# Norm sums of a DeltaNet head in four column strips, its 32x32 products of both chunks in turn, and z's last step emitted later

## The chip, the core and the metric

The kernel runs on one core of a Trainium2 chip. Such a core has a matrix engine (TensorE, PE in the profile; PEld is its loading of weights), a vector engine (VectorE, DVE), a scalar engine (ScalarE, ACT), a general one (GpSimd, POOL) and SyncE (SP), whose queue issues this kernel's DMAs. Each engine works through its own list of instructions in a fixed order and waits at an instruction whose operands are not there yet. The metric is the device time of one execution in microseconds (us), lower is better.

## The reference

One layer of a hybrid encoder block in float32, 1024 positions, width 1024: RMSNorm, one input projection, two mixers (a gated DeltaNet with 4 heads of 128, and a banded chunk attention), gates, output projection, a convolved feed-forward part, and a last RMSNorm. The change lies in the DeltaNet mixer:

```python
qa = l2norm(qa.reshape(b_, t_, GDN_HEADS, GDN_DK))
ka = l2norm(ka.reshape(b_, t_, GDN_HEADS, GDN_DK))
...
a_mat = beta[..., :, None] * jnp.einsum('nbhid,nbhjd->nbhij', k, k) * dec_strict
sol = lax.linalg.triangular_solve(a_mat + eye, rhs, left_side=True, lower=True)
...
oa = (rmsnorm(oa, gdn_norm_w[l]) * jax.nn.silu(za))
```

Positions are worked on in 16 chunks of 64. In each chunk a unit lower triangular 64x64 system is solved, and a state S of 128x128 is carried from chunk to chunk. The norm of q is not applied to q: since the output is normalised too, it is folded into the last RMSNorm, for which the sum of squares of q at each position is needed (sx in the kernel).

## The kernel before

**Stages.** All products are made as three matmuls of split operands (high and low parts), accumulated in PSUM. After the first loads (up to about 64 us) comes the DeltaNet stage (to about 440 us), then attention, the branch products, the output projection and the feed-forward part. In the DeltaNet stage PE has two kinds of work: *fill*, the input projections (psph, 24 matmuls of 128x512 to a half tile of 512 positions, one weight tile of `load_w` for two halves), and the heads' own products.

**One head.** Two chunks of 64 lie in one tile of 128 partitions, so 8 pairs (NT = 8), with chunk e = 0 or 1 in partitions 64e to 64e+63. `gdn_prep` and `gdn_prep2` transpose k and v (psk, psv), make the decays, and the 64x64 products psG and psQ, with the two chunks of a pair in two strips of 64 columns of the array, alternately. `gdn_solve` inverts the four 32x32 diagonal blocks on DVE, 31 dependent steps on tmp and Zt; the result goes to HBM (dZ) and comes back by four loads, one for each block, into the tile zt. `gdn_apply` (line 541) makes the remaining 32x32 block of each chunk's inverse: Z11 is a transposed copy, psB1 a product of 32x32 for each pair, copied by ACT to B1, psZ21 a second product, copied by ACT into zt. Then come psW and psU, with zt as operand. `gdn_chain` carries the state through 16 steps: psws, then U on DVE, then pss, then S on DVE; after every second step pso and O.

**q's norm.** `gdn_qnorm` (line 610) squares q on ACT (sqq, 128 x 8 x 128) and puts eight small matmuls (psn, one column each, sqq as weights) into the list `side`; `proj_half` issues one of them after each three psph. `gdn_qnorm2` copies psn to sx with two ACT copies. `gdn_rms` (line 627) uses sx on DVE (line 634) and scales O; `gdn_out` transposes O (psoT), multiplies by z and stores to dO.

**z.** `gdn_z` (line 597) makes silu of the output gate, by halves e: psph times rb on DVE (line 604), tanh on ACT (zth, line 605), and a last step on DVE, (zth + 1) x zs (line 606).

**The order.** The program is traced head by head (from line 665), the head's own work at high priority; a scheduler then sets each engine's order by priorities and by when it expects operands. The tables APP, QN, GFILL, OUT and others at the top of the file say at which half tile of the fill the apply, the norm sums and the output are emitted. `behind()` puts PE's instructions of a piece behind the last matmul traced with `mm`.

The page and the trace name tiles without trailing numbers: psB1 is psB, psZ21 is psZ, Z11 is Z, zt0 is zt.

## Time and profile before

| | |
|---|---|
| time, median of 3 runs | 1549.16 us (1548.48 to 1549.85) |
| the profiled execution's own time | 1549.47 us |
| its span, first to last instruction | 1547.7 us |
| mean granted clock of PE over the span | 0.997 |
| DeltaNet stage, 64 to 440 us: PE, DVE, ACT, POOL busy | 370.10, 257.95, 174.78, 115.96 us of 376 |

A line of the profile names the source line, the engine, the operation, and the tiles written and read (out<-in). In a list of waits the three numbers are the total in us, how often, and the longest. In a timeline a line gives start and duration in us, and in square brackets idle time of the engine just before and what ended it; equal neighbours are merged (x16). Matmuls are pipelined, so their durations overlap, and the distance of their starts is what they cost.

### The profile page before, as it was taken

To read this page: it belongs to the slowest core of one execution; us is meant where nothing else is said; L and a number is where in the kernel's file an instruction comes from. 1 tells how busy PE (TensorE), PEld (TensorE's weight loads), DVE (VectorE), ACT (ScalarE), POOL (GpSimd) and SP (SyncE) were. 2 spreads that over 40 slices of the span, in tenths; PEclk is the share of its full clock that TensorE was granted. 3 is DMA by queue.
4 is the path that set the end of the run, shared out by engine and by line. 5 is a ranking of instruction groups with operands and counts; after the bars stand their busy time and mean duration, and the time that the engine had idled before them with its cause. 6 is when DMAs were issued, how large, how long until landed. Compare 5 with 4: busy or idle time off the path is not lost.

```text
span 1547.7 us, 21371 instructions
## 1 busy us (share of the span) xinstructions
PE 1517.9 (98%) x7687; PEld 1245.4 (80%) x7687; DVE 1091.1 (70%) x2146; ACT 716.4 (46%) x1408; POOL 640.8 (41%) x603
## 2 busy tenths in 40 slices
PE   8999999999999999999999999999999999999997
PEld 6878787877778888887887888888888888878886
DVE  7775867948436877866554567777777777797886
ACT  7644526363225665754232245444444444443344
POOL 3633323312132112111320269877777776233253
PEclk9999999999999999999999999999999999999999
DMA  8122131222131101114553213333333332875523
GB/s 301 31 64 83 45 103 32 64 71 82 49 126 50 37 23 59 37 55 138 173 168 122 95 56 116 117 102 103 102 102 103 102 102 76 277 253 164 178 89 141
DMA packets 74507, 162.04 MB, mean 105 GB/s; under 512 B 15649, under 2 KB 16929, under 8 KB 74401
## 3 DMA queue, kind: packets, MB, share of 16 engines
q1 hardware_dynamic: 74400, 160.68, 31.4%
q8 instruction: 60, 0.98, 0.3%
q14 instruction: 47, 0.38, 0.1%
HBM read 120.55 MB, written 40.11 MB: 104 GB/s over the span
## 4 chain that ended last, share of the span: by engine, by line
PE 54%; DVE 1%; DMA 1%; issue 0%; ACT 0%; POOL 0%; POOLq 0%; SPq 0%; DVEq 0%; ACTq 0%
PE psd L52 9%; PE psph L52 8%; PE pb L52 8%; PE pa L52 5%; PE psout L52 5%; PE pc L52 5%; PE psd L1511 4%; PE pb L1156 4%; PE pa L1156 3%; PE pc L1156 3%; PE pso L52 1%; PE pst L1044 0%; PE psp L877 0%; DMA tb<-dG 0%; DMA woraw<-w_out 0%
## 5 line engine op out<-in xcount | busy, mean ns | idle before, releaser
L84 POOL TENSOR_TENSOR wlo<-wraw,whi 128x256 fp32r<-128x256 f32 x196 | 157.3, 832 | 441.6 <-ACT whi L81 268.7
L52 PE MATMUL psph<-BH,whi 128*128 128x512 f32 x688 | 280.4, 407 | 7.9 <-ACT BH L225 5.2
L52 PE MATMUL psph<-BL,whi 128*128 128x512 f32 x688 | 276.0, 401 | 0.1
L52 PE MATMUL psph<-BH,wlo 128*128 128x512 f32 x688 | 275.5, 400 | 0.0
L52 PEld LDWEIGHTS psph<-BH,whi 128*128 128x128 f32 x688 | 130.7, 190 | 30.1 <-ACT BH L225 5.6
L1170 POOL TENSOR_TENSOR ol<-wraw,oh 128x512 fp32r<-128x512 f32 x110 | 150.5, 1386 | 6.6 <-ACT oh L1170 6.5
L52 PEld LDWEIGHTS psph<-BL,whi 128*128 128x128 f32 x688 | 130.6, 190 | 22.9 <-DVE BL L226 2.1
L52 PEld LDWEIGHTS psph<-BH,wlo 128*128 128x128 f32 x688 | 130.5, 190 | 22.7
L1170 POOL TENSOR_TENSOR al<-araw,ah 128x1024 fp32r<-128x1024 f32 (+1 forms) x28 | 69.4, 2481 | 132.9 <-ACT ah L1170 108.0
L52 PE MATMUL psd<-wdl,ah 128*128 128x512 f32 (+1 forms) x311 | 120.6, 388 | 1.4 <-DVE wdl L1170 1.4
L1170 POOL TENSOR_TENSOR wraw<-wraw 128x512 f32<-128x512 f32 x86 | 119.2, 1386 | 4.9
L1511 PE MATMUL psd<-wdh,al 128*128 128x512 f32 (+1 forms) x311 | 120.4, 387 | 0.0
L52 PE MATMUL psd<-wdh,ah 128*128 128x512 f32 (+1 forms) x311 | 119.4, 387 | 0.0
L1170 ACT CAST oh<-wraw 128x512 fp32r<-128x512 f32 x110 | 67.8, 620 | 103.9 <-POOL wraw L1170 103.8
L1170 DVE TENSOR_TENSOR wdl<-W,wdh 128x512 fp32r<-128x512 f32 x77 | 95.0, 1272 | 27.6 <-ACT wdh L1170 27.5
L81 ACT CAST whi<-wraw 128x1024 fp32r<-128x1024 f32 (+2 forms) x61 | 55.3, 907 | 79.5 <-PE psph L52 66.0
L1170 ACT CAST ah<-araw 128x1024 fp32r<-128x1024 f32 (+1 forms) x39 | 40.6, 1040 | 107.1 <-PE psd L52 52.8
L1170 POOL TENSOR_TENSOR gl<-wraw,gh 128x512 fp32r<-128x512 f32 x42 | 56.2, 1342 | 68.7 <-ACT gh L1170 68.7
L52 PEld LDWEIGHTS psd<-wdl,ah 128*128 128x128 f32 x311 | 58.4, 188 | 14.2 <-DVE wdl L1170 2.2
L1156 PE MATMUL pa<-BH,gh 128*128 128x512 f32 x176 | 68.6, 389 | 0.0
L52 PE MATMUL pa<-BH,gl 128*128 128x512 f32 x176 | 68.5, 389 | 0.0
L52 PE MATMUL pa<-BL,gh 128*128 128x512 f32 x176 | 68.5, 389 | 0.0
(343 smaller groups left out, 3802.6 us busy)
## 6 DMA issues: line engine op xcount, KB each, us to landing
wraw<-w_up SPq DMA_DIRECT2D x44, 512.0 KB, 5.0
wraw<-w_tiles SPq DMA_DIRECT2D x42, 512.0 KB, 3.5
araw<-dA SPq DMA_DIRECT2D x77, 256.0 KB, 3.0
dA<-yu SPq DMA_DIRECT2D x33, 512.0 KB, 3.1
W<-w_down SPq DMA_DIRECT2D x44, 256.0 KB, 4.5
xt<-x SPq DMA_DIRECT2D x16, 512.0 KB, 4.8
dG<-gt SPq DMA_DIRECT2D x16, 512.0 KB, 2.8
ta<-dG SPq DMA_DIRECT2D x16, 256.0 KB, 3.0
```

What stands on the lines that cost most here:

```text
L52: last["mm"] = nc.tensor.matmul(*args, **kw).ins
L81: nc.scalar.copy(hi, src)
L84: nc.gpsimd.tensor_tensor(out=lo[:, k:k + 2], in0=src[:, k:k + 2], in1=hi.bitcast(F32)[:, k:k + 2], op=ALU.subtract)
L1156: i = nc.tensor.matmul(ps, wh[:, k], xh[:, k], start=start and k == 0, stop=False, **kw)
L1170: return lambda *args, **kw: tc.keep_in_program_order(f(*args, **kw))
L1511: i = nc.tensor.matmul(ps, al[:, j, ts], wh[:, es], start=False, stop=stop, **kw)
```

## The change

**Norm sums.** In place of eight products with sqq as weights and a single moving column there are four with 32 columns of ones as weights and 256 columns of sqq moving, each into its own strip of 32 PSUM partitions (psn is 128 x 256; all 32 rows of a strip are alike). They are one entry of `side`, issued together. ACT copies psn to sn, which shares the buffer of the tile B1; one DMA stores a row of each strip to HBM (dN), and two DMAs load it back, position by position, to sx (64 partitions x 8 single floats each).

**32x32 products.** `gdn_apply` now makes both chunks' transposes first, then the psB1 products of both chunks in turn, both copies, the psZ21 products in turn, both copies. The four loads of zt are issued in the order of blocks 1, 3, 0, 2.

**z.** The last step of a half is emitted later: that of e = 0 after the tanh of e = 1, that of e = 1 after the first half tile of the fill behind it.

The tile `ones` goes, and `mhalf` is wider.

```diff
-        for b in range(4):
+        for b in (1, 3, 0, 2):
             r = slice(b * 32, (b + 1) * 32)
             nc.sync.dma_start(zt[r, :, r], dZ[b].rearrange("n a c -> a n c"))
...
-        for e in range(2):
-            r0 = slice(e * CH, e * CH + 32)
-            r1 = slice(e * CH + 32, (e + 1) * CH)
+        rr = [(slice(e * CH, e * CH + 32), slice(e * CH + 32, (e + 1) * CH)) for e in range(2)]
+        for r0, r1 in rr:
             nc.vector.transpose(out=Z11[r0], in_=zt[r0, :, r0])
-            for p in range(NT):
+        for p in range(NT):
+            for r0, r1 in rr:
                 mm(psx1[r0, p * 32:(p + 1) * 32], nL[r1, p, 0:32], zt[r1, p, r1], start=True, stop=True)
+        for r0, r1 in rr:
             nc.scalar.copy(B1[r0].rearrange("p n j -> p (n j)"), psx1[r0, 0:256])
-            for p in range(NT):
+        for p in range(NT):
+            for r0, r1 in rr:
                 mm(psx2[r0, p * 32:(p + 1) * 32], Z11[r0, p, :], B1[r0, p, :], start=True, stop=True)
+        for r0, r1 in rr:
             nc.scalar.copy(zt[r0, :, r1], psx2[r0, 0:256].rearrange("p (n j) -> p n j", j=32))
...
-            nc.vector.scalar_tensor_tensor(out=zs[:, s], in0=th, scalar=1.0, in1=zs[:, s], op0=ALU.add, op1=ALU.mult)
+            if e:
+                c["zf"]()
+
+            def zf(th=th, s=s):
+                with behind():
+                    nc.vector.scalar_tensor_tensor(out=zs[:, s], in0=th, scalar=1.0, in1=zs[:, s], op0=ALU.add,
+                                                   op1=ALU.mult)
+
+            c["zf"] = zf
             yield
...
-        psn = psc.tile([P, 8], F32, tag="c", name="psn")
-        for p in range(NT):
-            side.append(lambda p=p: mm(psn[:, p:p + 1], sqq[:, p, :], ones, start=True, stop=True))
+        psn = psc.tile([P, 256], F32, tag="c", name="psn")
+
+        def sums():
+            for j in range(4):
+                mm(psn[j * 32:(j + 1) * 32], ones2[:, 0:32], sqq[:, 2 * j:2 * j + 2, :].rearrange("p n t -> p (n t)"),
+                   start=True, stop=True)
+
+        side.append(sums)
...
-        psn = c["psn"]
+        sn = gp.tile([P, 256], F32, tag="B1", name="sn")
+        nc.scalar.copy(sn, c["psn"])
+        dN = gd.tile([4, 256], F32, tag="dN", name="dN")
+        nc.sync.dma_start(dN, sn[0:P:32, :])
         sx = gp.tile([P, NT], F32, tag="sx", name="sx", bufs=2)
         for e in range(2):
-            nc.scalar.copy(sx[(1 - e) * CH:(2 - e) * CH], psn[e * CH:(e + 1) * CH])
+            nc.sync.dma_start(sx[(1 - e) * CH:(2 - e) * CH, :],
+                              bass.AP(tensor=dN.tensor, offset=dN.offset + e * CH, ap=[[1, CH], [P, NT]]))
...
             got = next(fill, "end") != "end"
+            if n == 0 and h >= 0:
+                cs[h]["zf"]()
```

**In PE's order**, first head, from the psph ahead of the first 32x32 products up to psW (psB and psZ are the two products, Z and B their operands), before:

```order
L52 MATMUL psph<-BH,wlo 128x512
L52 MATMUL psB_1273<-zt_289,nL 32x32 x8
L52 MATMUL psph<-BH,whi 128x512
L52 MATMUL psph<-BL,whi 128x512
L52 MATMUL psph<-BH,wlo 128x512
L52 MATMUL psZ_1275<-B_1274,Z_1272 32x32 x8
L52 MATMUL psB_1273<-zt_289,nL 32x32 x8
L52 MATMUL psph<-BH,whi 128x512
L52 MATMUL psph<-BL,whi 128x512
L52 MATMUL psph<-BH,wlo 128x512
L52 MATMUL psZ_1275<-B_1274,Z_1272 32x32 x8
```

and with the change:

```order
L52 MATMUL psph<-BH,wlo 128x512
L52 MATMUL psB_1271<-zt_287,nL 32x32 x16
L52 MATMUL psph<-BH,whi 128x512
L52 MATMUL psph<-BL,whi 128x512
L52 MATMUL psph<-BH,wlo 128x512
L52 MATMUL psZ_1273<-B_1272,Z_1270 32x32 x16
L52 MATMUL psph<-BH,whi 128x512
L52 MATMUL psph<-BL,whi 128x512
L52 MATMUL psph<-BH,wlo 128x512
L52 MATMUL psph<-BH,whi 128x512
L52 MATMUL psW<-zt_287,nKs 128x128 x4
```

Three groups among the psph have become two; the second and third head are alike. In the last head each of the two is torn: one psB alone, three psph, fifteen psB, three psph, one psZ alone, three psph, fifteen psZ. The psn rows were one after each third psph (in the last head all eight together); they are four together now in all heads. Between the last pso and the psoT of the last head stand 24 psph, where 16 stood.

**In DVE's order**, last head, from the end of the solve into the chain (the tile sx holds the sums, U and S are the chain's steps), before:

```order
L523 TENSOR_REDUCE Zt<-tmp 128x8
L176 TENSOR_TENSOR gt<-psph,rb 128x512
L634 TENSOR_SCALAR sx<-sx 128x8
L547 STREAM_TRANSPOSE Z_3812<-zt_289 32x256
L604 TENSOR_TENSOR zs<-psph,rb 128x512
L547 STREAM_TRANSPOSE Z_3812<-zt_289 32x256
L606 SCALAR_TENSOR_TENSOR zs<-zth,zs 128x512
L584 TENSOR_TENSOR U<-psws,U 64x128
```

and with the change:

```order
L521 TENSOR_REDUCE Zt<-tmp 128x8
L174 TENSOR_TENSOR gt<-psph,rb 128x512
L544 STREAM_TRANSPOSE Z_3810<-zt_287 32x256 x2
L605 TENSOR_TENSOR zs<-psph,rb 128x512
L612 SCALAR_TENSOR_TENSOR zs<-zth,zs 128x512
L585 TENSOR_TENSOR U<-psws,U 64x128
L586 TENSOR_SCALAR O<-psws,eg 64x128
L590 SCALAR_TENSOR_TENSOR S<-S,eg,pss 128x128
L652 TENSOR_SCALAR sx<-sx 128x8
L585 TENSOR_TENSOR U<-psws,U 64x128
```

The operation on sx has moved behind the chain's first step; z's last step stands where it stood, right ahead of the first U. Of the eight places of z's last step (four heads, two halves), five stand at the same step of the chain as before, and the others one to three steps later.

**In SP's order**, last head, before (dZ and zt are the solve's result, dG a gate's store, wraw a weight tile):

```order
L531 DMA dZ<-Zt 128x256
L180 DMA dG<-gt 128x1024
L536 DMA zt_289<-dZ 32x8x32 x4
L92 DMA wraw<-w_tiles 128x1024 x2
L180 DMA dG<-gt 128x1024
```

and with the change:

```order
L529 DMA dZ<-Zt 128x256
L534 DMA zt_287<-dZ 32x8x32 x4
L178 DMA dG<-gt 128x1024
L90 DMA wraw<-w_tiles 128x1024
L638 DMA dN<-sn 4x256
L641 DMA sx<-dN 64x8x1 x2
L90 DMA wraw<-w_tiles 128x1024
L178 DMA dG<-gt 128x1024
```

The loads of zt have moved ahead of the gate's store, and the three new transfers stand between two weight loads.

## The prediction

> **What bounds the kernel now.** I read the page first, then the busy time by stage, then what TensorE (PE) waited for, and last the timeline of PE around the instructions that the change touches.

> ```profile
> PE 1517.9 (98%) x7687; PEld 1245.4 (80%) x7687; DVE 1091.1 (70%) x2146; ACT 716.4 (46%) x1408; POOL 640.8 (41%) x603
> 64.00:440.00 376.00, 370.10 (x2302) 298.55 (x2301) 257.95 (x669) 174.78 (x447) 115.96 (x165) 1.00 0.20 64
> PE pss L52 <- DVE U L584: 3.1, 5, 1.2
> ```

> The second line is the DeltaNet stage, where all of the change lies: 376 us long, PE busy for 370.10 of it, DVE for 257.95, the granted clock 1.00. The third is the longest wait of PE on another engine there: 3.1 us in five pieces. So PE is the bound, its order is fixed, and it hardly waits: microseconds of PE work that go there come off the end, as long as no wait grows in their place.

> Busy time of PE is a poor measure of what a matmul costs, since matmuls overlap (one psph lasts 0.39 us, but the next starts after 0.227). I therefore measure cost by starts: the time from the last ordinary psph ahead of a piece of work to the second psph behind it, less an interval for each psph in that stretch. The first fence gives the interval (PE alone, start and duration in us; 66 intervals lie between its last two lines).

> ```profile
> 102.22 0.39 PE L52 MATMUL psph<-BH,wlo 128*128 128x512 f32 x1
> 102.45 0.28 PE L52 MATMUL psn<-ones,sqq 128*128 128x1 f32 x2
> ...
> 109.34 0.40 PE L52 MATMUL psph<-BL,whi 128*128 128x512 f32 x1
> ...
> 111.85 0.39 PE L52 MATMUL psph<-BH,whi 128*128 128x512 f32 x1
> ...
> 126.81 0.39 PE L52 MATMUL psph<-BH,whi 128*128 128x512 f32 x1
> ```

> The interval is (126.81 - 111.85) / 66 = 0.227 us.

> **The norm sums: what goes.** In the first head eight psn products lie among 23 intervals: 109.34 - 102.22 = 7.12, less 23 x 0.227 = 5.22, leaves 1.90 us, 0.24 each, for a product with a single moving column: the load of its 128 columns of weights is what is paid. The order of heads two and three is the same. In the last head the eight stand in a row:

> ```profile
> 385.70 0.39 PE L52 MATMUL psph<-BH,wlo 128*128 128x512 f32 x1
> 385.92 1.84 PE L52 MATMUL psn<-ones,sqq 128*128 128x1 f32 x16
> 387.62 0.48 PE L52 MATMUL psph<-BH,whi 128*128 128x512 f32 x1
> 387.94 0.39 PE L52 MATMUL psph<-BL,whi 128*128 128x512 f32 x1
> ```

> 387.94 - 385.70 - 2 x 0.227 = 1.79 us. Removed in all: 3 x 1.90 + 1.79 = 7.49. (The second line also shows that one float32 product is two records: eight give x16.)

> **The 32x32 products: what goes.** First head, PE alone:

> ```profile
> 127.26 0.39 PE L52 MATMUL psph<-BH,wlo 128*128 128x512 f32 x1
> 127.58 0.69 PE L52 MATMUL psB<-zt,nL 32*32 32x32 f32 x16
> ...
> 128.54 0.40 PE L52 MATMUL psph<-BL,whi 128*128 128x512 f32 x1
> 128.77 0.39 PE L52 MATMUL psph<-BH,wlo 128*128 128x512 f32 x1
> 129.09 0.59 PE L52 MATMUL psZ<-B,Z 32*32 32x32 f32 x13
> 129.50 0.21 PE L52 MATMUL psB<-zt,nL 32*32 32x32 f32 x1
> 129.52 0.19 PE L52 MATMUL psZ<-B,Z 32*32 32x32 f32 x1
> ...
> 130.45 0.39 PE L52 MATMUL psph<-BL,whi 128*128 128x512 f32 x1
> ...
> 131.00 0.69 PE L52 MATMUL psZ<-B,Z 32*32 32x32 f32 x16
> ```

> The first group of eight costs 128.54 - 127.26 - 0.45 = 0.83. The middle sixteen cost 130.45 - 128.77 - 0.45 = 1.23. The last eight look like the first (0.69 for x16): 0.83. Together 2.89 us a head. Within a group a record starts every (0.69 - 0.19) / 15 = 0.033 us, so 16 records are 0.53 of the 0.83, and 0.30 is the price of entering and leaving such a group.

> The middle lines hold the key. In program order all eight psZ products (rows and columns 0 to 31) stand ahead of psB's second eight (another corner of the array). Yet a psB starts at 129.50, before psZ at 129.52: where two corners have work in the queue, they run abreast, each at its own pace. With the chunks alternating, 32 records take 16 steps: 16 x 0.033 + 0.30 = 0.83 for psB, and the same for psZ: 1.66 a head, a saving of 1.23. In the last head the order tears each group in two, one product alone and fifteen behind the next three psph: 2 x (2 x 0.033 + 0.30 + 15 x 0.033 + 0.30) = 2.32, a saving of 0.57. Sum: 3 x 1.23 + 0.57 = 4.26 us. Bounds: nothing saved if corners did not overlap, which those lines exclude, and a little more if the groups' entries shrink.

> **The norm sums: what comes.** Four products now, each 128 rows by 32 columns of weights with 256 moving columns, into four column strips. No such form is in this trace; the nearest are these (first two lines: two strips of 64 columns taken alternately; last two: full width, 128 moving columns).

> ```profile
> 71.61 0.92 PE L52 MATMUL psG<-kf 128*64 128x64 f32 x24
> 72.36 1.10 PE L52 MATMUL psQ<-WQ,kf 128*64 128x64 f32 x32
> ...
> 132.42 1.05 PE L52 MATMUL psW<-zt,nKs 128*128 128x128 f32 x8
> 133.31 1.06 PE L52 MATMUL psU<-Vs,zt 128*128 128x128 f32 x8
> ```

> A full-width record of 128 columns takes (133.31 - 132.42) / 8 = 0.111 us, so one of 64 would take 0.056; psG takes (72.36 - 71.61) / 24 = 0.031. Two strips therefore run abreast almost without loss. A record of 256 columns takes 0.22. Four strips abreast: 2 x 0.22 + 0.30 = 0.74 us a head. Two abreast: 4 x 0.22 + 0.30 = 1.18. One after another: 8 x 0.22 + 0.30 = 2.06, a small loss. I take 0.90, nearer to the first, since psG shows no sign of a limit at two; it is charged four times, 3.60. The sums net 7.49 - 3.60 = 3.89 us saved, between -0.8 and 4.5.

> [...]

> **The transposes of the last head.** In the order, 24 psph now stand between the last pso and psoT of the last head, where 16 stood. These are PE's timeline there, and an answer on the tile psoT (engine and line waited for, us, times):

> ```profile
> 437.53 2.35 PE L649 MATMUL psoT<-ident,O 128*128 128x128 f32 x8
>   ACT O L641: 1.2, 7
> ```

> PE waited 1.2 us in seven pieces for ACT to scale O. Eight more psph, 1.8 us, are ahead of it now, so I count 1.2 as gained; it is between 0 and 1.2.

> **z's last step.** All waits of that step, and one of them on DVE and what it did to PE:

> ```profile
> DVE zs L606 <- ACT zth L605: 4.7, 7, 1.4
> 347.94 0.69 DVE L606 SCALAR_TENSOR_TENSOR zs<-zth,zs 128x512 f32<-128x512 f32 x1 [1.37 <-ACT zth L605]
> 349.02 0.49 PE L52 MATMUL pss<-U,Kd 128*128 128x128 f32 x2 [1.19 <-DVE U L584]
> ```

> The step waits on DVE for ACT's tanh, the chain's U queues behind it, and PE stands for 1.19. That is the wait the edit is about. But in the scheduled order the step stands at the same step of the chain as before in five of its eight places, the one above included. I take 0, between 3 gained (nearly all of the 3.1 above) and 1.4 lost (the longest of its waits).

> **The new path of the sums.** Each head adds an ACT copy (in place of two smaller ones), a store dN and two loads sx on SP's queue, dN waiting for ACT and sx for dN. Behind them on SP stand the next gate store and weight load. PE is not in this path; the DVE operation on sx is. Medians to landing of the nearest transfers, and a copy of ACT:

> ```profile
> dZ<-Zt SPq DMA_DIRECT2D x4, 128.0 KB, 1.7
> zt<-dZ SPq DMA_DIRECT2D x16, 32.0 KB, 2.1
> 394.90 0.36 ACT L550 COPY B<-psB 32x256 f32<-32x256 f32 x1
> ```

> By these, sx is there 1.7 + 2.1 = 3.8 us after the copy, 0.4 to 0.8 more for the second issue. In the first three heads the DVE operation on sx stands about where it stood, among solve steps. In the last head the copy waits for the tile B1 until psZ is read, and the DVE operation stands behind the chain's first step: three copies (1.1) and 4.4 make 5.5, while PE has 4 psph (0.9), 16 psW and psU (16 x 2 x 0.111 = 3.6) and a chain step (1.1) to do: 5.6. That is a tie. I charge 1.0 us for this and for the Z11 transposes that now get the last two of zt's four loads; bounds 0 and 3.

> **Sum.** -3.9 - 4.3 - 1.2 + 0 + 1.0 = -8.4 us. The profiled execution took 1549.47 us (span 1547.7); it would be 1541.1, and it lies 0.3 over the median of 1549.16: **1540.8 us**.

> **Rivals.**
> *Strips do not run four abreast.* If records start strictly in order, a strip's second record has to wait for its first and holds the next strip back: five steps, 5 x 0.22 + 0.30 = 1.40 a head, 4 x 0.50 = 2.0 more than I charge: 1542.8. One strip at a time gives 1540.8 + 4 x (2.06 - 0.90) = 1545.4. For it: no form with four strips in the trace. Against: psG, and the psB at 129.50.
> *The work saved comes back as waits.* DVE is busy for 258 of 376 us, and a faster PE reaches the chain's U, the solve's zt and the weights sooner. For it: five waits for U already, in a fixed order. Against: they add up to 3 us. It would return most of the 8 us: 1547 to 1550.
> *sx lands late, slower.* Its elements are single floats, 512 to a load. On DVE the operation on sx stands ahead of the chain's second U in the last head and ahead of solve steps in the others, so lateness passes to PE. To turn 8.4 gained into over 3.1 lost it must hold PE for 11.5 us: sx would land 12 us late in the last head alone, or 6 late in two heads. Then 1553. For it: nothing in the trace has such elements. Against: zt's, of 32 floats, land after 2.1. [...]

> **Numbers.** 0.2%, 3.1 us, is about what a measurement here can tell from no change. Forecast (1537.5 to 1543) 0.60; strips not abreast (1542.5 to 1546) 0.19; given back 0.15; sx late 0.06. The range 1537.5 to 1545.5 reaches over most of the second case and leaves about 0.22 out. Faster takes the first two cases, 0.79; same is the third, 0.15; slower the fourth, 0.06.

> **What would show it.** In the new profile: psn from one psph to the second behind it at about 0.74 (abreast), 1.2 or 2.1; psB and psZ x32 in about 0.7 us each; psoT of the last head near 1.0; the wait of zs on zth still near 4.7; the DVE operation on sx with a wait under 1 us. I am wrong if PE's waits for U, zt or psph grow by more than 3 us, or psn costs over 2 us.

## The result and the profile after

The changed kernel takes 1541.59 us (median of 6 runs, 1540.31 to 1542.62), the kernel before 1549.43 on the same chip (6 runs, 1548.48 to 1550.10): ratio 0.9948, 95% interval 0.9937 to 0.9958, 7.8 us faster. The forecast was 1540.8.

The profiled execution's span is 1540.1 us against 1547.7. First the page's line on the engines.

```profile
PE 1507.2 (98%) x7655; PEld 1236.0 (80%) x7655; DVE 1089.6 (71%) x2145; ACT 714.7 (46%) x1404; POOL 642.0 (42%) x603
```

Then the row of the busy times by stage for the same window, which now holds some 9 us of what used to come behind the DeltaNet stage.

```profile
64.00:440.00 376.00, 369.29 (x2308) 295.34 (x2308) 259.70 (x675) 174.70 (x445) 124.54 (x182) 1.00 0.23 70
```

PE lost 10.7 us of work and is still busy for 98%. Since a window cut by time mixes stages now, I compare the same matmul in both: PE's timeline before, at the 181st and the 1381st psph,

```profile
65.54 0.39 PE L52 MATMUL psph<-BH,whi 128*128 128x512 f32 x1
...
447.90 0.39 PE L52 MATMUL psph<-BH,whi 128*128 128x512 f32 x1
```

and after:

```profile
65.89 0.39 PE L52 MATMUL psph<-BH,whi 128*128 128x512 f32 x1
...
439.34 0.39 PE L52 MATMUL psph<-BH,whi 128*128 128x512 f32 x1
```

The stretch between them, "the stage" from here on, took 382.36 us and takes 373.45: 8.91 less, where the prediction's sum was 8.4 for all. Later 1.56 of it is given back, in the last products (psd), which took 210.74 us from the start of the last pb matmul to the start of PE's last matmul and now take 212.30.

**The norm sums**, first head, PE's timeline after:

```profile
102.58 0.39 PE L52 MATMUL psph<-BH,wlo 128*128 128x512 f32 x1
102.90 0.64 PE L52 MATMUL psn<-sqq,ones 128*32 128x256 f32 x8
103.47 0.50 PE L52 MATMUL psph<-BH,whi 128*128 128x512 f32 x1
103.81 0.39 PE L52 MATMUL psph<-BL,whi 128*128 128x512 f32 x1
```

By starts: 103.81 - 102.58 - 0.45 = 0.77 us, the same in all four heads. Eight records in 0.64 us, where one alone of 256 columns would take 0.22 by the prediction's estimate: four strips abreast. The single records' starts say it directly: four start within 0.02 us, at 102.901, 102.908, 102.914 and 102.921, and the other four 0.24 later, which I read as the first and second records of the four strips.

**The 32x32 products**, first head:

```profile
128.08 0.39 PE L52 MATMUL psph<-BH,wlo 128*128 128x512 f32 x1
128.40 0.69 PE L52 MATMUL psB<-zt,nL 32*32 32x32 f32 x32
129.02 0.50 PE L52 MATMUL psph<-BH,whi 128*128 128x512 f32 x1
129.36 0.40 PE L52 MATMUL psph<-BL,whi 128*128 128x512 f32 x1
129.60 0.39 PE L52 MATMUL psph<-BH,wlo 128*128 128x512 f32 x1
129.92 0.71 PE L52 MATMUL psZ<-B,Z 32*32 32x32 f32 x32
130.56 0.50 PE L52 MATMUL psph<-BH,whi 128*128 128x512 f32 x1
130.90 0.40 PE L52 MATMUL psph<-BL,whi 128*128 128x512 f32 x1
```

32 records now take the 0.69 us that 16 took: 0.83 and 0.85 by starts, 1.67 to 1.72 a head, 2.39 in the torn last one.

**The transposes of the last head**, which took 2.35 us:

```profile
430.26 1.03 PE L667 MATMUL psoT<-ident,O 128*128 128x128 f32 x8
```

**The new path of the sums.** The last head, where a tie was expected, in the timelines of SP and DVE:

```profile
390.34 0.54 SPq L638 DMA_DIRECT2D dN<-sn  x1
391.99 1.28 SPq L641 DMA_DIRECT2D sx<-dN  x2
...
395.03 0.35 DVE L590 SCALAR_TENSOR_TENSOR S<-S,eg,pss 128x128 f32<-128x128 f32 x1 [0.19 <-PE pss L52]
395.30 0.17 DVE L652 TENSOR_SCALAR sx<-sx 128x8 f32<-128x8 f32 x1
```

and, from the answer on the tile sx, the time from issue to landing, which the trace has for four of its eight loads:

```profile
DMA to landing us min/median/max: 2.4/2.5/2.6
```

The second load is issued at 392.64; its own landing is not in the trace, and by that median it lands at about 395.1. DVE reaches its operation at 395.30 and shows no wait: by this estimate there were about 0.2 us to spare.

**New waits.** In the first head PE waits twice for DVE's products of the gates (gt), which free the psph buffers. PE's timeline after, then DVE's after around the first:

```profile
114.73 0.50 PE L52 MATMUL psph<-BH,whi 128*128 128x512 f32 x1 [0.58 <-DVE gt L174]
...
120.74 0.47 PE L52 MATMUL psph<-BH,whi 128*128 128x512 f32 x1 [0.23 <-DVE gt L174]
...
113.30 0.39 DVE L519 TENSOR_TENSOR tmp<-Zt,Lr 128x184 f32<-128x184 f32 x1
113.73 0.35 DVE L521 TENSOR_REDUCE Zt<-tmp 128x8 f32<-128x192 f32 x1
114.00 0.68 DVE L174 TENSOR_TENSOR gt<-psph,rb 128x512 f32<-128x512 f32 x1
```

and DVE's before:

```profile
112.93 0.39 DVE L521 TENSOR_TENSOR tmp<-Zt,Lr 128x184 f32<-128x184 f32 x1
113.24 0.68 DVE L176 TENSOR_TENSOR gt<-psph,rb 128x512 f32<-128x512 f32 x1
```

DVE is in the solve's 31 steps there without a pause. gt stands one operation later in its order than before, and PE comes sooner: 0.75 and 0.39 us over the usual interval of starts, 1.14 in sum, none before. (Up to the second psph behind each wait, as the other terms are measured, it is 0.86 and 0.47, 1.33 in sum.)

In the last products PE waits for wdl. After:

```profile
1334.28 2.62 POOL L1190 TENSOR_TENSOR al<-araw,ah 128x1024 fp32r<-128x1024 f32 x1 [2.94 <-ACT ah L1190]
...
1334.58 3.47 DVE L1190 TENSOR_TENSOR wdl<-W,wdh 128x512 fp32r<-128x512 f32 x2
...
1337.50 0.50 PE L52 MATMUL psd<-wdl,ah 128*128 128x512 f32 x1 [1.25 <-DVE wdl L1190]
```

and before, where the same pair ran ahead of POOL's al:

```profile
1343.63 1.29 DVE L1170 TENSOR_TENSOR wdl<-W,wdh 128x512 fp32r<-128x512 f32 x2
...
1345.15 2.63 POOL L1170 TENSOR_TENSOR al<-araw,ah 128x1024 fp32r<-128x1024 f32 x1 [4.77 <-ACT ah L1170]
1345.62 2.71 DVE L1170 TENSOR_TENSOR wdl<-W,wdh 128x512 fp32r<-128x512 f32 x1
```

Beside POOL's al, DVE's pair takes 3.47 us in place of 1.29. The load of araw, on which al hangs, landed 3.61 us after its issue, 5.43 before. The two smaller waits for wdl that follow (0.90 and 0.44 us) are not new: before has them too, 0.92 and 0.46.

### The profile page after: what moved, and what is told of

Read it like the earlier page. It is cut to its first block, busy times and chain, and to the rows that moved or that the text cites. A ratio compares the mean times of both kernels' runs of the same rounds, so it can differ in the third digit from the quotient of the medians.

```text
span 1540.1 us, 21321 instructions
## 1 busy us (share of the span) xinstructions
PE 1507.2 (98%) x7655; PEld 1236.0 (80%) x7655; DVE 1089.6 (71%) x2145; ACT 714.7 (46%) x1404; POOL 642.0 (42%) x603
## 4 chain that ended last, share of the span: by engine, by line
PE 53%; DVE 2%; DMA 1%; issue 1%; ACT 1%; POOL 0%; SPq 0%; POOLq 0%; DVEq 0%; ACTq 0%
PE psd L52 8%; PE psph L52 8%; PE pb L52 7%; PE psout L52 5%; PE pa L52 5%; PE pc L52 5%; PE psd L1531 4%; PE pb L1176 4%; PE pa L1176 3%; PE pc L1176 2%; DVE wdl L1190 1%; PE pso L52 1%; DVE yu L1190 1%; PE pst L1064 0%; PE psp L897 0%
## 5 line engine op out<-in xcount | busy, mean ns | idle before, releaser
L52 PE MATMUL psph<-BH,whi 128*128 128x512 f32 x688 | 278.1, 404 | 8.7 <-ACT BH L223 5.3
L52 PE MATMUL psph<-BL,whi 128*128 128x512 f32 x688 | 276.8, 402 | 2.4 <-DVE BL L224 2.4
L52 PE MATMUL psph<-BH,wlo 128*128 128x512 f32 x688 | 274.3, 399 | 0.0
L52 PEld LDWEIGHTS psph<-BH,whi 128*128 128x128 f32 x688 | 130.3, 189 | 34.7 <-ACT BH L223 5.3
L52 PEld LDWEIGHTS psph<-BL,whi 128*128 128x128 f32 x688 | 130.7, 190 | 24.0 <-DVE BL L224 2.9
L52 PEld LDWEIGHTS psph<-BH,wlo 128*128 128x128 f32 x688 | 130.4, 190 | 23.0
L52 PE MATMUL psd<-wdl,ah 128*128 128x512 f32 (+1 forms) x311 | 120.7, 388 | 2.6 <-DVE wdl L1190 2.6
L52 PE MATMUL psd<-wdh,ah 128*128 128x512 f32 (+1 forms) x311 | 119.4, 387 | 0.0
L52 PEld LDWEIGHTS psd<-wdl,ah 128*128 128x128 f32 x311 | 58.4, 188 | 15.8 <-DVE wdl L1190 3.9
L1176 PE MATMUL pa<-BH,gh 128*128 128x512 f32 x176 | 68.6, 389 | 0.0
L52 PE MATMUL pa<-BH,gl 128*128 128x512 f32 x176 | 68.5, 389 | 0.0
L52 PE MATMUL pa<-BL,gh 128*128 128x512 f32 x176 | 68.5, 389 | 0.0
```

Source lines behind the costliest of these rows:

```text
L52: last["mm"] = nc.tensor.matmul(*args, **kw).ins
L1176: i = nc.tensor.matmul(ps, wh[:, k], xh[:, k], start=start and k == 0, stop=False, **kw)
```

## The experiments

Theory A was that the parts add up, and that what comes back comes in the first head and the last products. The rivals: that the sums or z's step gained something by way of the chain, that the path over HBM costs, that the strips ran abreast only in that one order. Times are medians beside runs of the kernel before on the same chip (1548.68 us for the first four, 1548.49 for the next four, 1548.76 for the three behind them, 1548.34 for the last). Stage and last products are read from one profile each, as above.

| run | us | ratio to before, 95% interval | stage | last products |
|---|---|---|---|---|
| sums alone | 1546.58 | 0.9986 (0.9978 to 0.9995) | 379.53 | 212.73 |
| 32x32 products alone | 1541.83 | 0.9957 (0.9944 to 0.9969) | 376.53 | 210.97 |
| z's step alone | 1549.52 | 1.0004 (0.9995 to 1.0013) | 382.39 | 211.07 |
| all but z's step | 1540.50 | 0.9948 (0.9935 to 0.9960) | 373.54 | 212.26 |
| round trip through dO | 1541.43 | 0.9953 (0.9940 to 0.9965) | 373.46 | 212.57 |
| first swap of ah and wdh | 1542.39 | 0.9962 (0.9948 to 0.9975) | 373.45 | 215.53 |
| other orders of the products | 1540.92 | one run | 376.00 | 210.74 |
| first head's sums later | 1541.48 | one run | 374.32 | 211.57 |
| sixteen DMAs | 1538.99 | 0.9943 (0.9929 to 0.9957) | 373.53 | 210.96 |
| second swap of ah and wdh | 1540.86 | 0.9945 (0.9933 to 0.9958) | 373.39 | 211.87 |
| the whole change again | 1540.42 | 0.9945 (0.9932 to 0.9957) | 373.45 | 211.30 |
| before, with twelve DMAs more | 1548.28 | 0.9996 (0.9987 to 1.0005) | 382.64 | 210.43 |

**The sums alone.** The diff's parts for mhalf, ones, psn, sn, dN and sx, on the kernel before.

```diff
-            side.append(lambda p=p: mm(psn[:, p:p + 1], sqq[:, p, :], ones, start=True, stop=True))
+        side.append(sums)
```

> Only the norm sums are changed. Theory A (the parts add up, and the first head is paced by DVE): the four heads' sums cost 0.77 us each in place of 1.90 or 1.79, so PE's work falls by 4.4; of that 1.1 comes back in the first head, where PE then waits for DVE's gate products (gt) among the solve steps; 3.3 us faster than before, and the last head's psoT still costs 2.35. Rival B (nothing comes back, or what comes back belongs to the other edits): 4.4 faster, no wait for gt. Rival C (the new path over HBM costs something): under 2.5 faster, with a wait of the DVE operation on sx.

The stage is 2.83 us shorter, the time 2.1 us. PE's timeline shows the wait for gt (0.60 and 0.23 us idle) and the last head's psoT as slow as before:

```profile
112.26 0.50 PE L52 MATMUL psph<-BH,whi 128*128 128x512 f32 x1 [0.60 <-DVE gt L174]
...
118.26 0.47 PE L52 MATMUL psph<-BH,whi 128*128 128x512 f32 x1 [0.23 <-DVE gt L174]
...
432.55 2.34 PE L656 MATMUL psoT<-ident,O 128*128 128x128 f32 x8
```

Theory A by the stage, 0.5 short of its 3.3, of which the longer measure of the gt waits explains 0.2. Rival C's size (under 2.5) came true in the time, but not its reason: DVE shows no wait for sx. In this profile the last products are 2.0 us longer, and the part ahead of the stage is 2.2 shorter; that part lay between 63.4 and 68.6 us in the profiles here and moves with the execution, so the time alone does not tell A from C.

**The products alone**, with the order of zt's loads.

```diff
-        for b in range(4):
+        for b in (1, 3, 0, 2):
...
-            for p in range(NT):
+        for p in range(NT):
+            for r0, r1 in rr:
                 mm(psx1[r0, p * 32:(p + 1) * 32], nL[r1, p, 0:32], zt[r1, p, r1], start=True, stop=True)
```

> Only the 32x32 products and the order of zt's four loads are changed. Theory A: 4.0 us of PE work go (1.2 in each of three heads, 0.5 in the torn one), and since PE's order then has 24 psph instead of 16 ahead of the last head's psoT, another 1.2 for that wait: 5.2 us faster, no wait for gt in the first head. Rival B (the psoT wait went because the sums became shorter): 4.0 faster, psoT still 2.35. Rival D (a faster apply only reaches a wait for zt or U sooner): under 3 faster, with PE's waits for U or S over 6 us in sum.

Stage 5.83 us shorter, time 6.85: a little more than A's 5.2. No wait for gt, and psoT is short without the new sums:

```profile
431.86 1.04 PE L652 MATMUL psoT<-ident,O 128*128 128x128 f32 x8
```

So the 1.3 us of psoT belong to this edit: 24 psph stand between the last pso and them in this kernel, 16 in that of the sums alone. B falls; D too, with 4.1 us of waits for U and S. What the order of zt's loads does by itself was not tried.

**z's step alone, and all but z's step.** The diff's two parts with zf, alone on the kernel before, and left out of the whole change.

```diff
-            nc.vector.scalar_tensor_tensor(out=zs[:, s], in0=th, scalar=1.0, in1=zs[:, s], op0=ALU.add, op1=ALU.mult)
+            if e:
+                c["zf"]()
```

> Only z's last step is emitted later. Theory A: no difference that can be measured, between 0.7 faster and 0.5 slower; DVE's waits of zs for zth stay between 3.5 and 5, PE's waits for U near 3. Rival E (the step was what held the chain): 1.5 to 3 us faster, PE's waits for U under 1.5.

> The whole change without the step of z. Theory A: the same as the whole change within what can be told, 7.5 to 9 us faster than before, by the stage's times 8.4 to 8.9. Rival E: 1.5 to 3 us less gained, so 5 to 7 faster.

Stage +0.03 us with it alone, and 373.54 against 373.45 without it: nothing in either direction. Rival E falls.

**Other orders of the same products.** Turns of 1, 2, 4, 8 products in psB by head, of 8, 4, 2, 1 in psZ; the sums in halves and quarters.

```diff
+        gB, gZ = (1, 2, 4, 8)[c["h"]], (8, 4, 2, 1)[c["h"]]
+        def turns(g):
+            return [(p, rr[e]) for b in range(0, NT, g) for e in range(2) for p in range(b, b + g)]
...
+            w = (256, 128, 128, 64)[c["h"]]
+            jk = [(j, k) for j in range(4) for k in range(0, 256, w)]
+            if c["h"] == 2:
+                jk.sort(key=lambda x: x[1])
```

> The same products in other orders, a form for each head. psB takes turns between the two chunks after 1, 2, 4, 8 products in heads one to four, psZ after 8, 4, 2, 1. The sums are whole in head one (4 products of 256 columns), in halves strip by strip in head two, in halves strip after strip in turn in head three, in quarters strip by strip in head four. Theory A (a corner or strip goes on by itself, but PE looks only about four records past the one that is held up): turns after 2 cost 0.85 to 0.95, after 4 about 1.05, after 8 about 1.25 in place of 0.83; sums in head two 1.1 to 1.7, in head three 0.8 to 0.9, in head four 1.5 to 2. Rival B (it looks past any number): 0.83 and 0.77 to 0.9 in all forms. Rival C (strict order, and the strips of the whole change only began together by chance of their order): turns after 2 already cost 1.2.

PE's timeline: psB in turns of 2, psB in turns of 4, psZ in turns of 8, then the sums in halves strip by strip and in quarters strip by strip.

```profile
223.03 0.71 PE L52 MATMUL psB<-zt,nL 32*32 32x32 f32 x32
...
312.50 0.89 PE L52 MATMUL psB<-zt,nL 32*32 32x32 f32 x32
...
127.80 1.09 PE L52 MATMUL psZ<-B,Z 32*32 32x32 f32 x32
...
192.25 0.66 PE L52 MATMUL psn<-sqq,ones 128*32 128x128 f32 x16
...
379.54 1.39 PE L52 MATMUL psn<-sqq,ones 128*32 128x64 f32 x32
```

By starts: turns of 2 cost 0.85 and 0.88, of 4 1.02 and 1.03, of 8 1.22; the sums 0.80 in halves strip by strip, 0.78 in halves in turn, 1.53 in quarters. B and C fall. A holds but for the halves strip by strip, expected at 1.1 or more: the limit is not four records in all, but four to a strip (last section).

**The first head's sums three half tiles later.**

```diff
-QN = (7, 5, 7, 5)
+QN = (10, 5, 7, 5)
```

> The whole change with the first head's sums three half tiles later, behind PE's two waits for gt. Theory A (DVE, busy with solve steps and the gt among them without a pause, paces that stretch): PE still waits for gt, 1.0 to 1.8 us in sum, and the first head ends between 0.2 earlier and 0.4 later than in the whole change. Rival B (the waits belong to the place of the sums): no wait for gt, 0.8 to 1.1 us faster.

PE waits for gt three times, 1.4 us idle in sum where the whole change has 0.8, once more than there (at 107.76, where the sums had stood ahead), and the sums now lie behind the waits:

```profile
114.00 0.50 PE L52 MATMUL psph<-BH,whi 128*128 128x512 f32 x1 [0.53 <-DVE gt L174]
...
119.94 0.47 PE L52 MATMUL psph<-BH,whi 128*128 128x512 f32 x1 [0.17 <-DVE gt L174]
...
120.81 0.64 PE L52 MATMUL psn<-sqq,ones 128*32 128x256 f32 x8
```

The stage is 0.87 us longer: 0.71 of it in the first head, more than A's 0.4, and the rest in the third. B falls. DVE paces PE from there to the end of the solve. Counted from the stage's start, PE was 0.77 us ahead of the whole change without the sums at the 323rd psph of the trace, level with it after the first wait, and 0.64 behind once the sums had come: they cost nothing where the change has them, and nearly the full price behind it. (DVE also waits 3.7 us for sx here, later in the first head; PE's lag does not grow there.)

**The last products: who makes wdl late.** Five kernels. The round trip through an unused part of dO, so that nothing is added in HBM:

```diff
-        dN = gd.tile([4, 256], F32, tag="dN", name="dN")
-        nc.sync.dma_start(dN, sn[0:P:32, :])
+        dN = dO[c["h"], 0]
+        nc.sync.dma_start(dN.rearrange("(j t) -> j t", t=256), sn[0:P:32, :])
```

> The whole change, but the sums' round trip goes through a part of dO that is still unused, so that no tile is added in HBM and what lies behind keeps its place there; as many DMAs as in the whole change. In the three profiles with the new sums the load of araw at the start of the last products lands after 3.6 us (two of them looked at), and PE then waits 1.2 to 1.5 us for wdl there; in the three without them it lands after 5.0 to 5.4 and the wait is not there. Theory P (the place in HBM does it): landing again after 5 us, that wait of PE gone, 1.4 us faster than the whole change. Theory Q (the number of DMAs ahead does it): landing after 3.6 us, the wait there, the time of the whole change.

Landing after 3.63 us, PE idle there for 1.17 us: the place in HBM is not it. ACT's wdh ahead of its ah, at two places:

```diff
     down_step(1)
-    prep_a(2)
     prep_w(2)
+    prep_a(2)
```

> The whole change, but at the start of the last products ACT makes wdh ahead of ah, so that POOL's subtraction al starts about 1.2 us later, behind DVE's first two wdl. Theory A (the 1.2 to 1.5 us of PE's wait there come from POOL's al running at the same time as DVE's wdl, which then takes 2.9 us in place of 0.7): the first wdl pair back to 1.3 us, that wait of PE gone, 1.2 to 1.5 us faster than the whole change, 9 to 10 faster than before. Rival B (wdl is late for its operands): the wait stays, no difference.

```diff
     down_step(3)
-    prep(3)
+    prep_w(3)
+    prep_a(3)
```

> The whole change, with ACT's wdh ahead of its ah one step later than in the earlier swap, at the al that really lies over the wdl pair in question. Theory A (POOL's al and DVE's wdl slow each other where they overlap): al starts about 1.2 us later, the first wdl of the pair takes 0.7 again, PE's first wait there falls from 1.2 to about 0.5; what the later al then lies over takes as much longer, so the whole is between 0.7 faster and 2 slower than the whole change. Rival B (wdl is late for its operands): wdl still 1.7 us each, the wait unchanged.

Both moved an al that lies ahead of the one in question, whose ah waits for its load and not for ACT. The first made PE's wait longer (1.91 us idle), the second left it (1.21). In the first the pair in question does take 1.28 us, as theory A expected, but it starts 3.4 us later behind the last pb matmul: the moved al holds the wdl pair ahead of it (4.51 us in place of 3.48), and the al in question now lies over the four yu between, which take 5.07 us in place of 2.85. So it is the end of the pair that PE waits for, whichever of DVE's instructions lose the time. (The first swap's profile is of the slowest of its five executions, 1545.30 us, and its 215.53 is high for that.) The second shows the overlap in another pair. In the whole change the second half of that pair starts 0.5 us behind the start of POOL's al and takes 2.88 us; here it starts ahead of al, and the two halves take 1.28:

```profile
1326.24 1.28 DVE L1190 TENSOR_TENSOR wdl<-W,wdh 128x512 fp32r<-128x512 f32 x2
...
1326.99 2.79 POOL L1190 TENSOR_TENSOR al<-araw,ah 128x1024 fp32r<-128x1024 f32 x1 [0.63 <-ACT ah L1190]
```

Sixteen DMAs more in place of twelve, and the whole change once more beside it:

```diff
-        for e in range(2):
+        for e, n0, n1 in ((0, 0, NT), (1, 0, 4), (1, 4, NT)):
```

> The whole change with one of the two loads of sx split in two, so that 16 DMAs are added in place of 12. In all seven profiles with the new sums so far the second araw load at the start of the last products landed after 3.0 to 3.7 us, in the three without them after 5.0 to 6.3, wherever dN lies. Theory R (the kernel's DMAs take eight semaphores in turn; twelve more shift that turn by four, sixteen more leave it as it was): landing after 5.0 us or more again, DVE's wdl pair at 1.3 us, no wait of PE at the first psd of that place; 0.5 to 1.5 us faster than the whole change. Theory Q (any DMAs added ahead): 3.0 to 3.7 us, the wait there, no difference from the whole change.

> The whole change once more, unchanged, on the chip of the two others. All theories: 7 to 9 us faster than before; the DeltaNet stage 8.9 us shorter, within 0.1; sums at 0.77 us a head. Whether PE's two later waits for wdl in the last products (0.9 and 0.4 in the first profile) are there again tells whether they belong to the kernel or to the execution.

Landing after 3.50 us, so R falls (its eight semaphores in turn are in the traces: 57 issues to each before, 58 or 59 after); PE is idle there for 0.89 us. The medians lie 1.4 us apart, but the two intervals overlap nearly whole, so the sixteen are not shown to be faster. The whole change again has the stage to 0.01 us, PE's idle 1.25 us and of the two later waits only the smaller (0.47): the other one varies with the execution, and with it the last products, 211.30 us here and 212.30 in the first profile. Last, the kernel before with twelve small DMAs more:

```diff
+        for i in range(3):
+            nc.sync.dma_start(dO[c["h"], i:i + 1, 0:16], c["sqq"][i:i + 1, 0, 0:16])
```

> The kernel before, with three stores of 64 bytes to HBM added at each head's norm sums, twelve in all, that nothing waits for; PE's, DVE's and ACT's order are those of before. Theory Q (DMAs added ahead, whatever they carry, change when the araw load at the start of the last products lands): second araw there after 3.0 to 3.7 us, DVE's wdl pair at 2.9 us each record's end to end in place of 1.3 for both, a wait of PE there of 0.8 to 1.5; the time between the same as before and 1.5 us slower, since the kernel's later waits there may shrink in turn. Rival S (it belongs to the sums, or to the products that now come earlier): landing after 5.0 us or more, no such wait, the time of before. Both: the DeltaNet stage as before, 382.4 us within 0.2.

No wait at that place, the pair 1.29 us, the time of before: Q falls. The landing itself is not in this trace. Here al starts 16.0 us behind the last pb matmul, between before's 16.8 and the whole change's 14.7; in both of those it starts 1.2 us behind the landing, so by estimate the load landed some 5.2 us after its issue, as rival S has it.

What stands: in the four profiles without the new sums PE has no such wait and the last products take 210.4 to 211.1 us; in the eight with them (the swaps left out) PE is idle there for 0.9 to 1.5 us and they take 210.7 to 212.7, 1.0 more in the mean, which is also the distance of the whole change's own two profiles. The wait is shown to come with the new sums; its price in time is known less well. Why the load lands sooner with the new sums stays open. No kernel here is shown to beat the whole change.

## Why the prediction was right, point by point

**PE bounds, and work that goes comes off the end**: right; 8.91 us in the stage.

**The norm sums**, 3.9 expected: 7.49 - 4 x 0.77 = 4.41 of PE work. Four strips do run abreast, at the lower bound of 0.74 rather than the 0.90 charged; the rivals with five steps (1.40) or one strip at a time (2.06) are out. But 1.14 of it came back in the first head. That is the step that failed: the sum took each microsecond of PE work at full value, and asked only of zt, U and the weights whether they would be late, not of gt, which stands among DVE's solve steps and frees psph's buffers. Moving those sums behind that stretch showed that their 0.77 us of PE work are free where they stand.

**The 32x32 products**, 4.26 expected: 11.44 - 7.45 = 3.99, by starts. The torn last head costs 2.39 for 2.32, and the groups of before were 2.86 in place of 2.89.

**psoT**, 1.2 expected: 1.3 (2.20 less 0.89, by starts), and the products alone bring it.

**z's step**, 0 expected: 0.03 and 0.09. The wait that was to stay near 4.7 us did so with the step alone; in the whole change it is 4.0, and the same without the step:

```profile
DVE zs L612 <- ACT zth L606: 4.0, 5, 1.3
```

**The new path and the transposes**, 1.0 charged: DVE did not wait for sx in the profile above. It did for 0.3 us in the whole change's second profile (second head) and for 0.4 with the sixteen DMAs (last head), and the stages of these two are within 0.1 us of the first. The prediction's 5.5 and 5.6 us for the last head's tie were close: the operation is met or missed there by less than half a microsecond. The charge was wrong, and gt's 1.14, which it did not hold, has nearly the same size: that part of the sum was right by luck.

Together -4.41 + 1.14 - 3.99 - 1.31 = -8.57; the stage gives -8.91. The other 0.3 (0.5 with 1.33 for gt) are not located: PE's idle time for U fell from 3.1 to 2.8 us, but that for S rose from 1.1 to 1.5.

**Given back as waits**, the rival: it had the right idea at the wrong places. The waits for gt took 1.1 us, and the last products, 900 us behind the stage, 1.6 in this profile. It did not return most of the gain.

**sx late, slower**: not seen; the waits for sx above did not reach the stage's time.

The profiled execution ended 7.6 us earlier: 8.91 in the stage, 0.35 lost ahead of it and 1.56 in the last products, 0.3 gained between them and 0.3 behind PE's last matmul. The forecast's 8.4 lay between stage and end because one thing that it charged did not happen and two that did were not in it.

## What to carry to other kernels

Small matmuls into different strips or corners of the array are cheap when the order takes turns between them after one or two products (0.83 to 0.89 us here, 1.22 after eight), and the distance of starts, not busy time, tells what they cost. Before PE work is taken off, look in that stretch for the engine that frees PE's buffers: where it is busy without a pause, as DVE here in the solve, a part of the saving is not paid out (1.14 of 4.41 us here). Try the parts alone: here their stages add up to within 0.3 us, and one of the three edits was worth nothing.

## What the runs showed of the hardware

**POOL and DVE.** In the profile of before, 24 wdl start while an al of POOL runs, and each ends 0.54 to 0.56 us behind it. In the lines shown, al ends at 1345.15 + 2.63 = 1347.78 and wdl at 1345.62 + 2.71 = 1348.33, 0.55 us later, which is nearly the 0.68 us of a wdl by itself. The longest of the 24 takes 2.88 us. I read these times as a wdl that gets little done until al has ended; what in the chip makes it so, no run here shows. It goes the other way too. In the whole change one al starts at 1377.96, while DVE works on W; two wdl that start behind it, at 1378.49 and 1379.09, take their 0.68 us each, and al takes 4.07 us (2.40 is its median) and ends 2.3 behind the second: there it is POOL's instruction that takes longer, over three of DVE's instructions that follow each other without a pause.
